# A longer hand-fixed order of VectorE and ScalarE through two products, spatial turns ahead of the first logits, and one addition ordered behind a norm

## The chip, the cores and the metric

The kernel runs on one core of a Trainium2 chip. The metric is the device time of one execution in microseconds, as the median of several runs. TensorE (PE) multiplies matrices and transposes tiles into PSUM, VectorE (DVE), ScalarE (ACT) and GpSimd (POOL) do elementwise work, and SyncE (SP) issues most DMAs; ScalarE issues a few. Every engine works through its own queue in order and waits for others by semaphores.

## What is computed

A decoder block on a sequence of 1024 tokens of width 1024, in float32: a norm, one projection, two groups of heads beside each other (attention with a forget gate, and a causal spatial gating), an output projection, and a gated MLP of width 2816 with a short causal convolution.

```
xn = rmsnorm(h);  proj = xn @ w_in            # q, k, v, u, vg, forget gate
att = forgetting_attention(q, k, v, log_f)    # 8 heads of 64, causal
sg  = u * (tril(w_s) @ rmsnorm(vg) + b_s)     # in chunks of 128 tokens; u, vg = gelu(proj)
h = h + concat(att, sg) @ w_out
h = h + conv_ffn(rmsnorm(h))                  # (silu(g) * a) @ w_down behind a causal conv of width 3
out = rmsnorm(h)
```

## The kernel before

**Numbers.** TensorE multiplies fp32r values here. To hold float32 accuracy each operand is split into a high part (a cast, on ScalarE) and a low part (the value less the cast, on VectorE), and a product is three matmuls: high by high, high by low, low by high. Thus every operand costs ScalarE a cast and VectorE a subtraction before TensorE can start on it. `tsplit` (line 242) splits a weight tile into one of six buffers that are used in a ring (`RTAG`, line 196); `own` (207) splits an x tile and scales it by the norm's gain; `hl_of` (213) splits two x tiles at once; `tmul` (249) does the 12 matmuls of one 128-row step k of a product, and `tprod` (258) does four of these steps, each with its split.

**Products.** The large products are done in Strassen's manner in Winograd's form: 2x2 blocks, seven products instead of eight, with sums of blocks on either side. The x blocks and their sums are named B11, B21, B22 and T1 to T4; the weight sums S1 to S4. The first stage (lines 219 to 408) is the projection to u and vg. Its product results go to two sets of four PSUM banks, `B` and `S`, which are exchanged after T2. From there the order of TensorE is T3 (banks S), T1 (banks B, 48 matmuls), T4 (added into S), B22 (added into B), and then the value products of the second token half (`values_high`, line 472), the queries and keys (`qk_step`, 588).

- `ut[1]` is bank B (of T2) less `vgt[0]`, and has to be read before T1 overwrites B. `vgt[1]` is `ut[1] + S`, less B after T1.
- `gb[k]` holds two weight blocks; T1 takes their sum, T4 the second one alone.
- `tmp[j]` holds x differences. `tmp[j][0]` is the source of T1, `tmp[j][1]` that of T4 (after one more operation with x21, the `t2` lines), `tmp[j][2]` that of B22. `tmp[1][1]` and `tmp[1][2]` lie in the buffer that `vgt[1]` takes later.
- `squares(tt)` (line 317) loads a token tile from `xtok` on SyncE and has ScalarE add up its squares; two load buffers are used in turn. From the eight sums, `rstd1` (a square root on ScalarE, a reciprocal on VectorE) is made; it is needed by the gelus, and as `rb`, stored by ScalarE's DMA to `rbd` and loaded back as a row by SyncE, for the queries and keys.

**The order.** The program's instructions are placed in each engine's queue by a scheduler with its own cost model. The class `Line` (line 28) wraps ScalarE, VectorE and GpSimd: while `on` is true, every instruction of that engine is tied behind the one before it, so the engine keeps the written order; once it is off, later instructions are only tied behind the last of the fixed ones. In the kernel before, the order of ScalarE and VectorE is fixed from the start to B22's splits (line 365) and is free from there, so T1 and T4 with their splits are placed by the scheduler. A trace shows instructions of a fixed order at L51 and those after it at L44, whatever line called them.

**The spatial turns.** After attention's inputs are ready, the spatial gating (`spatial`, 722) leaves its output in `ut[0]` and `ut[1]`; the latter is multiplied by GpSimd (L752). `turn_sg(hf, c, ps)` (761) transposes four blocks of it on TensorE into one bank, and `sg_hi` and `sg_lo` split the result into `sgT` (tag G). Then a new PSUM pool has two buffers "L" of two banks each for logits: `logits_mm(h, j, ps)` (898, matmuls L907 and L908) computes query block j of a head, `logits_min` (912) reads it on VectorE and sets the buffer free, and `logits_exp` runs on ScalarE. `firsts` holds the buffers of blocks 7 and 6; block 5 takes that of block 7. `seq` fixes the order of TensorE here, and the fixed order of ScalarE and VectorE holds too.

**The second norm.** After attention, `wmm` (1174) does the output projection of one token tile, `hadd` (1186) adds the half result to the rest of the residual stream, which `hload` has loaded, `norm2` (1190) norms the tile, and `flip` (1207) transposes it (L1214) for the next product. The tiles come in the order 0, 4, 1, 5, 2, 3, 6, 7, and a tile is flipped after the next one's norm is written. The order of VectorE is free here.

## Time and profile before

| | us |
|---|---|
| median of 3 runs | 1063.64 |
| lowest and highest run | 1061.78, 1063.86 |
| profiled execution | 1064.82 |
| its span, first to last instruction | 1063.1 |
| TensorE busy | 1048.1 (99%) |
| VectorE busy | 886.9 (83%) |
| ScalarE busy | 571.2 (54%) |
| GpSimd busy | 234.5 (22%) |

A row of a list of instructions reads: start, busy time, engine, line, operation, tile written <- tiles read, shape, count, and in brackets the engine's idle time just before with what ended it. Rows of one kind in a row are merged, so the time of a row with x4 is that of four. Tile names are without their numbers: "wy" and "whl" are the ring of weight splits, "H", "V", "x" and "t" hold x operands, "pb" and "ps" are PSUM banks, "pl" the logits' buffers. A row of the waits names who waited, for whom, then the total, the times and the longest. A row of the stretches gives start:end, length, the busy time and instructions of PE, PE's weight loads, DVE, ACT and POOL, then PEclk, the TensorE clock granted (1.00 is full), the DMA share and GB/s.

### The profile page before, as it was taken

The page shows a single profiled execution, that of the slowest core. Times are in us where ns is not written, and L with a number is a line of the kernel's source. Part 1 is how long each engine was busy: PE and PEld are TensorE (multiplying, and loading weights), DVE is VectorE, ACT ScalarE, POOL GpSimd, SP SyncE. Part 2 cuts the span into 40 slices and gives each one's busy share as a digit, 9 for nine tenths or more (in the row PEclk, how much of TensorE's full clock was granted, in tenths as well). Part 3 has the DMA queues.
Part 4 walks back from the last instruction along what each step waited for, and adds up shares of the span by engine and source line. Part 5 has one row for each costly group of instructions (what it writes and reads, how often), then busy time and mean ns, then how long its engine had stood idle before and what let it go on. Part 6 is the DMA issues. An engine that isn't in the chain of part 4 may idle for free.

```text
span 1063.1 us, 14614 instructions
## 1 busy us (share of the span) xinstructions
PE 1048.1 (99%) x5156; PEld 881.9 (83%) x5156; DVE 886.9 (83%) x1297; ACT 571.2 (54%) x1013; POOL 234.5 (22%) x177
## 2 busy tenths in 40 slices
PE   9989999999999999999999999999999999999997
PEld 7978888988889887878888888888888888888885
DVE  6899697877877869998999989989898866997774
ACT  6667534465866846754434444444444544554653
POOL 0003141330420740153333433323321000000000
PEclk9999999999999999999999999999999999999999
DMA  9613365857565444223245323332322899333432
GB/s 338 201 28 113 104 172 155 228 156 193 152 180 159 139 158 169 75 84 108 90 149 176 132 100 100 109 108 80 129 100 77 291 331 304 115 100 99 142 119 96
DMA packets 67184, 155.78 MB, mean 147 GB/s; under 512 B 9028, under 2 KB 9748, under 8 KB 67112
## 3 DMA queue, kind: packets, MB, share of 16 engines
q1 hardware_dynamic: 65800, 154.82, 45.6%
q8 instruction: 40, 0.66, 0.3%
q14 instruction: 32, 0.26, 0.1%
q10 hardware_dynamic: 1312, 0.04, 0.1%
HBM read 111.96 MB, written 42.87 MB: 146 GB/s over the span
## 4 chain that ended last, share of the span: by engine, by line
PE 87%; DVE 7%; DMA 3%; ACT 2%; issue 1%; SPq 0%; DVEq 0%; ACTq 0%
PE k L1527 20%; PE qa L1269 11%; PE qc L1269 11%; PE qd L1269 10%; PE qb L1269 5%; PE ps L259 4%; PE pb L966 3%; PE pb L947 3%; PE pb L259 2%; PE qa L418 2%; PE qc L418 2%; PE qd L418 2%; PE pl L907 2%; PE pl L908 2%; PE pf L991 1%; PE pf L993 1%
## 5 line engine op out<-in xcount | busy, mean ns | idle before, releaser
L1527 PE MATMUL k<-whb,wha 128*128 128x512 f32 x924 | 209.8, 389 | 0.0
L1527 PEld LDWEIGHTS k<-whb,wha 128*128 128x128 f32 x924 | 173.4, 188 | 36.2 <-DVE wha L161 0.2
L1269 PE MATMUL qc<-xT,whb 128*128 128x512 f32 x540 | 129.9, 390 | 0.5 <-DVE u L1380 0.5
L1269 PE MATMUL qa<-xB,wha 128*128 128x512 f32 x528 | 127.2, 390 | 0.0
L1269 PEld LDWEIGHTS qc<-xT,whb 128*128 128x128 f32 x540 | 101.3, 188 | 22.0 <-DVE u L1380 0.9
L1269 PEld LDWEIGHTS qa<-xB,wha 128*128 128x128 f32 x528 | 98.8, 188 | 20.8 <-DVE wha L161 0.4
L155 ACT CAST wha<-sg 128x512 fp32r<-128x512 f32 x77 | 47.8, 622 | 97.0 <-PE k L1527 86.4
L155 ACT CAST whb<-sg 128x512 fp32r<-128x512 f32 x82 | 50.5, 617 | 87.1 <-PE qc L1269 68.7
L161 DVE TENSOR_TENSOR wha<-sg,wha 128x512 fp32r<-128x512 f32 x77 | 52.8, 688 | 40.0 <-ACT wha L155 39.9
L948 ACT CAST pt<-pb 128x512 fp32r<-128x512 f32 (+1 forms) x80 | 42.2, 544 | 43.1 <-PE pb L947 34.2
L1269 PE MATMUL qd<-xB,whb 128*128 128x512 f32 x264 | 63.9, 390 | 0.1
L1269 PE MATMUL qd<-xT,whb 128*128 128x512 f32 x264 | 63.6, 389 | 0.0
L161 DVE TENSOR_TENSOR whb<-sg,whb 128x512 fp32r<-128x512 f32 x82 | 57.7, 705 | 4.4 <-ACT whb L155 4.3
L1269 PE MATMUL qb<-xT,whb 128*128 128x512 f32 x252 | 60.8, 389 | 0.0
L1156 POOL TENSOR_TENSOR sg<-raw 128x512 f32<-128x512 f32 x20 | 30.2, 1512 | 136.7 <-DVE whb L161 75.7
L949 DVE TENSOR_TENSOR pt<-pb,pt 128x512 fp32r<-128x512 f32 (+1 forms) x80 | 48.8, 635 | 12.3 <-ACT pt L948 11.0
L1269 PEld LDWEIGHTS qd<-xB,whb 128*128 128x128 f32 x264 | 49.5, 188 | 10.8 <-DVE h L1388 0.5
L1269 PEld LDWEIGHTS qd<-xT,whb 128*128 128x128 f32 x264 | 49.6, 188 | 10.3
L1269 PEld LDWEIGHTS qb<-xT,whb 128*128 128x128 f32 x252 | 47.3, 188 | 9.8
L966 PE MATMUL pb<-pt,V 128*128 128x256 f32 x320 | 52.1, 288 | 0.3 <-DVE pt L949 0.2
L1159 POOL TENSOR_TENSOR sg<-sg,raw 128x512 f32<-128x512 f32 x20 | 33.3, 1664 | 64.4 <-DVE whb L161 64.4
L1157 POOL TENSOR_TENSOR sg<-sg,raw 128x512 f32<-128x512 f32 x20 | 34.8, 1742 | 50.7 <-issue 48.8
(404 smaller groups left out, 2287.0 us busy)
## 6 DMA issues: line engine op xcount, KB each, us to landing
raw<-wup SPq DMA_DIRECT2D x44, 512.0 KB
sg<-hx SPq DMA_DIRECT2D x77, 256.0 KB
hx<-hs SPq DMA_DIRECT2D x44, 256.0 KB
hx<-ca SPq DMA_DIRECT2D x35, 256.0 KB
xT<-wdn SPq DMA_DIRECT2D x28, 256.0 KB
x<-kd SPq DMA_DIRECT2D x24, 256.0 KB
A<-xtok SPq DMA_DIRECT2D x8, 512.0 KB
raw<-wqk SPq DMA_DIRECT2D x8, 512.0 KB
```

The source lines that it names most:

```text
L155: act.copy(h, src)
L161: return eng.tensor_tensor(out=l, in0=src, in1=f32(h), op=ALU.subtract)
L259: pe.matmul(banks[m], xs(n, xi, k)[:, ms], w[:, wi, :], start=(first and k == 0 and c == 0 and (own or m % 2 == 0)), stop=(k == 3 and c == ...
L418: pe.matmul(ps, w[:, wi, ks], xs(n, xi, k), start=(first and c == 0), stop=(c == 11), skip_group_check=True)
L947: seq(pe.transpose(ptr[:, c:c + P], tj[jj][:, k * P:(k + 1) * P], ident))
L948: casts.append(act.copy(pt[:, 0, 0:w], ptr[:, 0:w]))
L949: los.append(dve.tensor_tensor(out=pt[:, 1, 0:w], in0=ptr[:, 0:w], in1=f32(pt[:, 0, 0:w]), op=ALU.subtract))
L966: seq(pe.matmul(po[0][:, oo:oo + n], lhs, pt[:, s, o:o + n], start=(k == 0 and s == 0), stop=(s == 1 and half)))
L1157: pool.tensor_tensor(out=s[1], in0=s[0], in1=a11, op=ALU.add)
L1159: pool.tensor_tensor(out=s[3], in0=s[1], in1=a12, op=ALU.add)
L1269: pe.matmul(ps, w[:, wi, ks], xb[:, xi, k, :], start=(first and n == 0), stop=(n == 11), skip_group_check=True)
L1527: pe.matmul(banks[bk + m], xh[:, xi, ms], wh[:, wi, :], start=(first and p_ == 0 and n == 0), stop=(p_ == NP - 1 and n == 2), skip_group_c ...
```

## The change

The diff has four parts.

1. The fixed order of ScalarE and VectorE goes on through T1 to the splits of T4. In it the weight sums of `gb` come right after T3's splits, then T1's own splits, with squares(6) and squares(7) between them and the `ut[1]` subtractions ahead of the last of them, then the weight splits for T1, and with them the root for `rstd1`. The gelus of `ut[0]`, the `t2` operations and T4's splits follow, still fixed. The store to `rbd` and the load of `rb` come after the fixed order.
2. `ut[1] + S` is written to a new tile `mid` in the buffer of tag t3 instead of `vgt[1]`, ahead of T4's splits. B22's first half uses that same single buffer, so its split comes after `mid` has been read; B22's second half is split after the fixed order. The two `sum4` come there too.
3. All four turns of the second half of the spatial output come ahead of the logits of blocks 7 and 6, instead of two turns, block 7, two turns, block 6.
4. VectorE's `hadd` of tile 5 is tied behind the last operation of the norm of tile 1.

```diff
             tmul(S, tsplit(ua[k][:, 0, :]), "T3", k, True)
-        squares(5 + j)
-    squares(7)
-    XS["B22"] = xset(("t3", "t2"))
-    for j in range(2):
-        hl_of("B22", j, tmp[j][2])
-    act.on = dve.on = False
-    for m in range(4):
-        dve.tensor_tensor(out=ut[1][:, m, :], in0=B[m], in1=vgt[0][:, m, :], op=ALU.subtract)
+        if j == 0:
+            squares(5)
     for w in gb:
         dve.tensor_tensor(out=w[:, 0, :], in0=w[:, 0, :], in1=w[:, 1, :], op=ALU.add)
-    XS["T1"] = xset(("H", "H"))
+    XS["T1"], mid = xset(("H", "H")), sb("t3", [P, 4, 512])
+    for k in range(4):
+        if k == 3:
+            for m in range(4):
+                dve.tensor_tensor(out=ut[1][:, m, :], in0=B[m], in1=vgt[0][:, m, :], op=ALU.subtract)
+        own("T1", tmp[k // 2][0][:, k % 2], k, k)
+        if k in (1, 2):
+            squares(5 + k)
+    for k in range(4):
+        tmul(B, tsplit(gb[k][:, 0, :]), "T1", k, True)
+        if k == 1:
+            act.activation(rstd1, ss1, AF.Sqrt, bias=eps[:, 0:1], scale=1.0 / 1024)
+            dve.reciprocal(rstd1, rstd1)
+    for m in range(4):
+        gelu(ut[0][:, m, :], m)
+    for k in range(4):
+        t2 = tmp[k // 2][1][:, k % 2]
+        dve.scalar_tensor_tensor(out=t2, in0=xr("x21", k), scalar=gk(4 + k), in1=t2, op0=ALU.mult, op1=ALU.subtract)
+    for m in range(4):
+        dve.tensor_tensor(out=mid[:, m, :], in0=ut[1][:, m, :], in1=S[m], op=ALU.add)
+    XS["T4"] = xset(("V", "V"))
     for j in range(2):
-        for c in range(2):
-            own("T1", tmp[j][0][:, c], 2 * j + c, 2 * j + c)
-
-
-    act.activation(rstd1, ss1, AF.Sqrt, bias=eps[:, 0:1], scale=1.0 / 1024)
-    dve.reciprocal(rstd1, rstd1)
+        hl_of("T4", j, tmp[j][1])
+        for k in (2 * j, 2 * j + 1):
+            tmul(S, tsplit(gb[k][:, 1, :]), "T4", k, False)
+    act.on = dve.on = False
     rb = sb("t01", [P, 1024])
     act.dma_start(out=rbd.rearrange("a p -> p a"), in_=rstd1)
     sp.dma_start(out=rb, in_=rbd.rearrange("a b -> (a b)").unsqueeze(0).to_broadcast((P, 1024)))
-
-    tprod(B, lambda k: gb[k][:, 0, :], "T1", True)
-    for m in range(4):
-        gelu(ut[0][:, m, :], m)
+    XS["B22"] = xset(("t3", "t2"))
+    hl_of("B22", 1, tmp[1][2])
     sum4(2)
     sum4(3)
-    for m in range(4):
-        dve.tensor_tensor(out=vgt[1][:, m, :], in0=ut[1][:, m, :], in1=S[m], op=ALU.add)
...
     for m in range(4):
-        dve.tensor_tensor(out=vgt[1][:, m, :], in0=vgt[1][:, m, :], in1=B[m], op=ALU.subtract)
+        dve.tensor_tensor(out=vgt[1][:, m, :], in0=mid[:, m, :], in1=B[m], op=ALU.subtract)
+    hl_of("B22", 0, tmp[0][2])
     tprod(B, lambda k: ua[k][:, 1, :], "B22", False)
...
     for c in range(4):
         pts.append(turn_sg(1, c, bank()))
-        if c % 2:
-            logits_mm(0, 7 - c // 2, firsts[7 - c // 2])
+    for j in (7, 6):
+        logits_mm(0, j, firsts[j])
...
     def hadd(tt, hf, ps):
         o = slice(hf * 512, hf * 512 + 512)
-        dve.tensor_tensor(out=h2[tt][:, o], in0=ps, in1=h2[tt][:, o], op=ALU.add)
+        x = dve.tensor_tensor(out=h2[tt][:, o], in0=ps, in1=h2[tt][:, o], op=ALU.add)
+        if tt == 5:
+            after(tc, x, normed[1])
```

The first `...` leaves out the removed lines with the `t2` operations, T4's splits and T4's product in their old place; `normed[tt]` holds the last VectorE operation of `norm2(tt)`.

More of the change, by code (lines that the diff above doesn't have):

```diff
@@ L380, in block_kernel @@
     sp.dma_start(out=rb, in_=rbd.rearrange("a b -> (a b)").unsqueeze(0).to_broadcast((P, 1024)))
-    tprod(B, lambda k: gb[k][:, 0, :], "T1", True)
-    for m in range(4):
-        gelu(ut[0][:, m, :], m)
+    XS["B22"] = xset(("t3", "t2"))
+    hl_of("B22", 1, tmp[1][2])
     sum4(2)
     sum4(3)
-    for m in range(4):
-        dve.tensor_tensor(out=vgt[1][:, m, :], in0=ut[1][:, m, :], in1=S[m], op=ALU.add)
-    for j in range(2):
-        t2 = tmp[j][1]
-        for c in range(2):
-            k = 2 * j + c
-            dve.scalar_tensor_tensor(out=t2[:, c], in0=xr("x21", k), scalar=gk(4 + k), in1=t2[:, c],
-                                     op0=ALU.mult, op1=ALU.subtract)
-    XS["T4"] = xset(("V", "V"))
-    for j in range(2):
-        hl_of("T4", j, tmp[j][1])
-    tprod(S, lambda k: gb[k][:, 1, :], "T4", False)
     wh = []
@@ L1172, in block_kernel @@
     xn = [None] * 8
+    normed = {}
     def wmm(tt, hf, ps, ks_):
@@ L1195, in norm2 @@
         dve.reciprocal(r, r)
-        dve.scalar_tensor_tensor(out=xn[tt], in0=h2[tt], scalar=r, in1=g2b, op0=ALU.mult, op1=ALU.mult)
+        normed[tt] = dve.scalar_tensor_tensor(out=xn[tt], in0=h2[tt], scalar=r, in1=g2b, op0=ALU.mult, op1=ALU.mult)
         sp.dma_start(out=h2d[tt], in_=h2[tt])
```

## The prediction, made before the result was known

> **What bounds the kernel now.** I read the head of the page first, then TensorE's waits, then the stretch around the longest of them.

> ```profile
> span 1063.1 us, 14614 instructions
> ...
> PE 1048.1 (99%) x5156; PEld 881.9 (83%) x5156; DVE 886.9 (83%) x1297; ACT 571.2 (54%) x1013; POOL 234.5 (22%) x177
> ```

> TensorE is busy for 1048.1 of 1063.1 us. The change removes no matmul, so it can save only TensorE's idle time (15.0 us in all, most of it at the two ends) and what slow clock follows from it. The list of who made TensorE wait shows which of that is within reach (total us, times, longest):

> ```profile
> PE ps L259 <- DVE wy L44: 3.1, 1, 3.1
> PE ps L122 <- DVE pad L133: 1.3, 1, 1.3
> PE ps L1214 <- DVE xn L1196: 0.9, 1, 0.9
> PE pb L947 <- DVE pt L949: 0.8, 2, 0.5
> PE pl L907 <- DVE G L51: 0.7, 1, 0.7
> ```

> Rows one, three and five are the three places that the diff touches: the start of product T1, the flip of token tile 1 after the second norm, and the first logits after the spatial turns. The stretches around the first one (start:end, length, busy times, then PEclk, the granted clock):

> ```profile
> 50.21:61.09 10.88, 10.88 (x50) 9.01 (x49) 7.78 (x12) 9.05 (x14) 0.00 (x0) 1.00 0.06 25
> 62.16:65.26 3.10, 0.00 (x0) 0.00 (x0) 3.10 (x7) 1.64 (x4) 0.00 (x0) 1.00 0.00 0
> 65.26:67.92 2.66, 2.66 (x8) 2.10 (x9) 2.66 (x5) 2.65 (x4) 0.00 (x0) 0.71 0.18 2
> 67.92:76.99 9.07, 9.07 (x37) 7.42 (x36) 8.26 (x13) 4.79 (x7) 0.00 (x0) 0.90 0.11 7
> 76.99:87.87 10.88, 10.88 (x49) 9.01 (x48) 10.88 (x15) 6.98 (x11) 3.97 (x4) 1.00 0.80 255
> ```

> T3 (48 matmuls) takes 10.88 us, T4 too. T1, between them, has the same 48 matmuls and takes 76.99 - 61.09 = 15.90. So the wait costs 15.90 - 10.88 = **5.02 us**, not 3.10: after it TensorE has a granted clock of 0.71 for 2.66 us and of 0.90 for 9.07 us, which is 0.29 x 2.66 + 0.10 x 9.07 = 1.68 us lost; the last 0.24 is the restart.

> Why T1 waits is read on VectorE, which is busy through the whole wait:

> ```profile
> 54.73 1.23 DVE L51 TENSOR_TENSOR t<-pt,t 128x1024 fp32r<-128x1024 f32 x1 [3.10 <-ACT t L51]
> 55.87 1.22 DVE L51 TENSOR_TENSOR t<-G,t 128x1024 fp32r<-128x1024 f32 x1
> 57.01 2.48 DVE L44 TENSOR_TENSOR A<-ps,G 128x512 f32<-128x512 f32 x4
> 59.40 2.49 DVE L44 TENSOR_TENSOR G<-G 128x512 f32<-128x512 f32 x4
> 61.81 1.41 DVE L44 SCALAR_TENSOR_TENSOR H<-pt,g,H 128x512 fp32r<-128x512 f32 x2
> 63.13 1.41 DVE L44 SCALAR_TENSOR_TENSOR H<-t,g,H 128x512 fp32r<-128x512 f32 x2
> 64.46 0.19 DVE L44 RECIPROCAL rstd<-rstd 128x8 f32<-128x8 f32 x1
> 64.57 0.64 DVE L44 TENSOR_TENSOR wy<-G,wy 128x512 fp32r<-128x512 f32 x1
> ```

> It sat idle from 51.63 to 54.73, then did B22's two splits (not needed before 87.87), the four ut[1] subtractions, the four weight sums, T1's four own splits, the reciprocal, and only then the weight split T1 waits for. ScalarE caused the idle time, in the fixed order, with the load for squares(7):

> ```profile
> 49.59 0.62 ACT L51 CAST wy<-raw 128x512 fp32r<-128x512 f32 x1
> 50.11 1.06 ACT L51 ACTIVATE A<-A 128x1024 f32<-128x1024 f32 x1
> 51.07 0.19 ACT L51 ACTIVATION_READ_ACCUMULATOR A<-A 128x1 f32 x1
> 52.61 1.06 ACT L51 ACTIVATE A<-A 128x1024 f32<-128x1024 f32 x1 [1.35 <-DMA A<-xtok]
> ```

> **The change, part by part.** *T1.* I put the new fixed order on the old clock. From the starts above, one of a row costs VectorE 0.60 us (four sums or subtractions in 2.39, or a split), 0.66 (an own split) and 1.14 (a 1024-wide split). T3's last split ends at 51.63 in both kernels. Then: sums of gb to 54.0; own splits 0 to 2 to 56.0; ut[1] subtractions to 58.4; own split 3 to 59.1; weight split of gb[0] to **59.7**. T3 ends at 61.09, so T1 finds everything ready with 1.4 us to spare; gb[1] follows at 60.3 and is needed at 61.09 + 2.72 = 63.8. ScalarE has to be ahead. Its last T3 cast ends at 50.1; own casts 0 and 1 (0.62 each) to 51.35, squares(6) to 52.4, own cast 2 to 53.0, squares(7) (load there at 52.6, issued as before, since squares(5) stays where it was) to 54.1, own cast 3 and the first two gb casts to 56.0. Each is before VectorE's use. So both the 3.10 us and the slow clock go: **-5.02**.

> What is late next? T4, which now begins at 71.97. VectorE from 59.7: three gb splits and the reciprocal to 61.6, four t2 operations to 64.3, four additions into mid to 66.7 (T3 is done by 61.5), T4's first 1024-wide split to 67.8, its first weight split to 68.4: 3.5 us early. On ScalarE these wait for the gelus, and those for the reciprocal:

> ```profile
> 65.10 1.28 ACT L44 ACT_TABLE_LOAD   x1 [1.46 <-DVE rstd L44]
> 66.39 2.56 ACT L44 ACTIVATE A<-A,rstd 128x512 f32<-128x512 f32 x4
> ```

> With the reciprocal at about 60.5, load and gelus end at 64.3, T4's first cast (two of 0.62 at most) at 65.5, before VectorE's 66.7. Then B22 at 82.85. Its first half must now wait until mid, which holds the one t3 buffer, has been read: T1's end at 72.2, four subtractions 2.4, a cast of up to 1.24, a split of 1.14, so 77.0 at the earliest; 5.9 us to spare. The buffers of the splits are a ring of six filled in the same order as before, so no split waits for another matmul.

> Queues: the rbd store moves behind the fixed order on ScalarE, and the load of rb on SyncE waits for it, with the wv loads behind:

> ```profile
> 64.68 0.39 ACTq L44 DMA_DIRECT2D rbd<-rstd  x1
> ```
> ```profile
> 74.03 0.33 SPq L380 DMA_DIRECT2D t<-rbd  x1
> 75.30 3.92 SPq L403 DMA_DIRECT2D G<-wv  x4
> ```

> 9.35 us lie from the store to the load of rb. With the store at about 68.5 the wv loads go out at about 78 to 82, some 3 us later than now, for values that TensorE takes up behind B22, now at 87.87 + 10.88 = 98.75, then at 93.7: hidden, and it would cost only the part of a delay beyond some 7 us. Bounds for the T1 part: a gain of 5.02 at most, and nothing if T4 or B22 takes the wait over.

> *Turns.* Transposes (L767), the first logits (block 7, 219.53) and the third (block 5, 222.26), with the pieces beside them on GpSimd and VectorE:

> ```profile
> 217.78 1.06 PE L767 MATMUL pb<-ident,A 128*128 128x128 f32 x8
> 219.53 0.50 PE L907 MATMUL pl<-x 128*128 128x512 f32 x1 [0.69 <-DVE G L51]
> ...
> 222.26 0.40 PE L907 MATMUL pl<-x 128*128 128x512 f32 x1
> ```
> ```profile
> 213.52 5.58 POOL L752 TENSOR_TENSOR A<-pt,A 128x256 f32<-128x256 f32 x8
> ```
> ```profile
> 220.76 1.28 DVE L51 CUSTOM_DVE_ANT_0 t<-pl,t,lim 128x1024 f32<-128x1024 f32 x1 [0.69 <-PE pl L908]
> ```

> The eight transposes that now stand between blocks 7 and 6 take up to 1.06 us and go into the gap of 0.69 ahead of block 7, so TensorE is through block 6 by about 0.8 us earlier. But block 5 takes the buffer of block 7, which is free only when VectorE's 1.28 us operation on block 7 is through, at 222.04, and that operation starts behind block 7, which hardly moves. Block 5 starts at 222.26 now, so the wait goes from the first block of L907 to the third. The turns of c = 3 also need GpSimd's eighth product, which ends at 219.10; TensorE gets there twelve transposes behind 217.78, at about 219.0 to 219.4, and that can push block 7 by 0.1 to 0.3 us. I take **0.0**, from -0.2 (222.26 becomes 222.1) to +0.3, nearest to what the buffer allows.

> *Addition.* At the second norm, TensorE then VectorE:

> ```profile
> 403.80 1.06 PE L1214 MATMUL ps<-ident,xn 128*128 128x128 f32 x8 [0.92 <-DVE xn L1196]
> ```
> ```profile
> 400.59 0.16 DVE L1195 RECIPROCAL ss<-ss 128x1 f32<-128x1 f32 x1
> 401.77 0.69 DVE L1188 TENSOR_TENSOR pt<-pb,pt 128x512 f32<-128x512 f32 x1 [1.02 <-DMA pt<-hpd]
> 402.38 1.27 DVE L1196 SCALAR_TENSOR_TENSOR xn<-pt,ss,g2b 128x1024 f32<-128x1024 f32 x1
> ```

> VectorE holds for hadd(5), which waits 1.02 us for its load, with the norm of tile 1 ready behind it. With the norm first it runs at 400.75 to 402.0, ahead of TensorE, which is free at 403.80 - 0.92 = 402.88; hadd(5) starts at 401.95, its load having landed, 0.18 later than now, while all that stands behind the pair starts about 1.0 us earlier. The gain on TensorE is 0.92 and up to 0.2 of restart, and no more than the 1.0 that VectorE gains, since flips and norms alternate from here to the next product: **-1.0** (bounds 0 and -1.1).

> Sum: -5.0 + 0.0 - 1.0 = -6.0. The profiled execution took 1064.82 us (its span 1063.1 and 1.7 around it), so 1058.8; the median of the runs, 1063.64, is 1.2 lower, which gives **1057.6 us**.

> **Rivals.** *The clock dips without the wait.* No other wait of this trace is above 1.3 us and none but this one has a clock under 1.00 behind it within the stages read, which speaks for the wait as the cause; but there is only this one case. If the dip stays, T1 gains only about 3.1 + 0.2 and the time is 1057.6 + 1.7 = 1059.3.
> [...]

> *VectorE in the fixed order is later than worked out* by 2 us or more (a semaphore's delay at each of some 25 steps). T1 has 1.4 us to spare, so a wait of about 1 us stays, or T4 gets it: half of the T1 part, 1060.1.

> *B22's first half is late (slower).* Behind the fixed order the program places VectorE's work freely, and VectorE was busy 10.88 of 10.88 us in T4's stretch. If over 5.9 us of other work (weight splits, square sums, the gate's reductions) stands ahead of mid's subtractions and B22's split, TensorE waits at 82.85, and a wait costs 5.02 / 3.10 = 1.6 per us with the clock. It eats the whole gain at 3.7 us of wait; from 5.1 us on the kernel is slower by over 0.2%: about 1066. Against it: mid's subtractions come ahead of the other work in the program, and what is left for that stretch is worth about 8 us.

> *Nothing changes:* T1's wait only moves to T4, 1063.

> **How the numbers follow.** Forecast 0.64 (its own range 1056.3 to 1058.9: the bounds of turns and addition, and the 1 us that the three runs lie from their middle); the clock 0.12 (1059.3); VectorE late 0.08 (1060.1); nothing 0.06 (1063); slower 0.10 (1066). A measurement of this kernel can tell about 0.2% (2.1 us) from no change. Faster: 0.64 + 0.12 + 0.08 = 0.84; same 0.06; slower 0.10. The range reaches over the first three cases: 1056.3 to 1061.0.

> **What would show it.** TensorE's 3.1 us wait at L259 for the wy split gone, T1 in about 10.9 us, granted clock 1.00 from 50 to 75 us, and every later stage 5.0 us earlier. At the turns, a wait of about 0.7 us at L907 for VectorE's minimum in place of the one for G. No wait of L1214 for xn at tile 1, and 1.0 us more between spatial turns and first up-projection. I am wrong if a product from T1 to B22 waits for VectorE, if the clock dips anyway, or if VectorE's free order after the fixed one lets a later product wait.

## The result, and the profile after

| | before | after |
|---|---|---|
| median of 6 runs each | 1062.71 us | 1058.90 us |
| lowest to highest | 1061.48 to 1064.18 | 1058.51 to 1059.72 |
| profiled execution, its span | 1064.82, 1063.1 | 1059.72, 1058.0 |

The ratio is 0.9965, with a 95% interval of 0.9952 to 0.9977: 3.7 us faster (2.4 to 5.1). The forecast was 1057.6 within 1056.3 to 1061.0, so the time lies in the range, 1.3 us above the forecast, and the gain is 3.7 us where 6.0 were worked out. Two things have to be explained: which parts brought it, and where the other 2.3 us are.

TensorE's waits in the changed kernel, in the form who waited, for whom, total us, times, longest:

```profile
PE ps L122 <- DVE pad L133: 1.3, 1, 1.3
PE pb L259 <- ACT wy L51: 1.0, 1, 1.0
PE pb L946 <- DVE pt L948: 0.8, 2, 0.5
PE pl L906 <- DVE mn L51: 0.6, 1, 0.6
PE pb L259 <- DVE wy L51: 0.3, 1, 0.3
PE pb L965 <- DVE pt L948: 0.2, 1, 0.2
PE qc L1271 <- ACT whb L155: 0.2, 1, 0.2
```

The 3.1 us for the wy split at T1 and the 0.9 us for xn at tile 1 are gone. The row of the logits now names the minimum (mn) in place of the split G. The two L259 rows are at the very first products (6.2 and 9.8 us after the start), where nothing was changed: in this one execution ScalarE waits 1.1 us for the first wuv load, for which it has no wait in the profile of before, and T3 begins at 51.24 us, 1.03 us later than in the profile of before. T3, T1 and T4 in the changed kernel, as stretches:

```profile
51.24:62.12 10.88, 10.88 (x49) 9.01 (x48) 10.88 (x20) 10.13 (x17) 0.00 (x0) 1.00 0.07 26
62.12:73.00 10.88, 10.88 (x49) 9.01 (x48) 10.88 (x16) 7.59 (x12) 0.00 (x0) 1.00 0.30 3
73.00:83.88 10.88, 10.88 (x49) 9.01 (x48) 10.53 (x15) 7.37 (x11) 1.50 (x2) 1.00 0.68 131
```

T1 now takes 10.88 us like its neighbours, at a granted clock of 1.00. VectorE in its fixed order, from T3's last split to T1's splits:

```profile
51.98 0.68 DVE L51 TENSOR_TENSOR wy<-raw,wy 128x512 fp32r<-128x512 f32 x1
52.58 2.49 DVE L51 TENSOR_TENSOR G<-G 128x512 f32<-128x512 f32 x4
54.99 1.41 DVE L51 SCALAR_TENSOR_TENSOR H<-pt,g,H 128x512 fp32r<-128x512 f32 x2
56.31 0.74 DVE L51 SCALAR_TENSOR_TENSOR H<-t,g,H 128x512 fp32r<-128x512 f32 x1
56.98 2.47 DVE L51 TENSOR_TENSOR A<-ps,G 128x512 f32<-128x512 f32 x4
59.37 0.74 DVE L51 SCALAR_TENSOR_TENSOR H<-t,g,H 128x512 fp32r<-128x512 f32 x1
60.03 0.68 DVE L51 TENSOR_TENSOR wy<-G,wy 128x512 fp32r<-128x512 f32 x1
```

There is no idle time in it, and T1's weight split ends at about 60.7, 1.4 us ahead of T1, the spare time that the prediction gave. (Other executions have more or less, as the section on the length of a wait shows.) The turns, TensorE first:

```profile
213.92 2.22 PE L766 MATMUL pb<-ident,A 128*128 128x128 f32 x16
215.89 0.48 PE L906 MATMUL pl<-x 128*128 128x512 f32 x1
...
218.46 0.50 PE L906 MATMUL pl<-x 128*128 128x512 f32 x1 [0.55 <-DVE mn L51]
```

All sixteen transposes come first and block 7 starts without a wait, but block 5 then waits 0.55 us. From the start of the first turns to block 5 it was 222.26 - 216.03 = 6.23 us before and is 218.46 - 212.17 = 6.29 now. The second norm, VectorE and then TensorE:

```profile
396.80 0.16 DVE L1197 RECIPROCAL ss<-ss 128x1 f32<-128x1 f32 x1
396.99 1.28 DVE L1198 SCALAR_TENSOR_TENSOR xn<-pt,ss,g2b 128x1024 f32<-128x1024 f32 x1
398.20 0.68 DVE L1229 TENSOR_TENSOR t<-xtB,ps 128x512 f32<-128x512 f32 x1
398.79 0.68 DVE L1230 TENSOR_TENSOR t<-xtB,xtB 128x512 f32<-128x512 f32 x1
399.40 0.68 DVE L1188 TENSOR_TENSOR pt<-pb,pt 128x512 f32<-128x512 f32 x1
```
```profile
398.43 1.07 PE L1216 MATMUL ps<-ident,xn 128*128 128x128 f32 x8
```

The norm comes right behind its reciprocal, the flip follows without a wait, and hadd(5) comes two operations later still.

Where the difference of the two profiled spans, -5.1 us, comes from, by the starts of the same products on TensorE: +1.03 from the first loads, -5.02 at T1, +0.13 up to the spatial turns, +0.06 at the turns, -0.8 from flips and norms to the first up-projections (436.91 to 432.33, where flip 0 had gone from 396.64 to 392.85), +0.7 in the second step of the up-projection and -1.2 in its third, where before a product waited 0.5 us for VectorE and restarted. The last two belong to the tie of hadd(5): all nine profiles of kernels with the tie have them, and none of the five without it. The first loads apart, the difference is -6.1 us, next to the -6.0 of the sum. So the sum was about right for the one execution that it was made from, though partly by luck, since the last two were not in it and nearly make up for a smaller gain at the flips. The kernel's other runs are not all like that one.

### The profile page after: what moved, and what is told of

Its sections match the earlier page's. It is cut to its first block, busy times and chain, and to the rows that moved or that the text cites. A ratio compares the mean times of both kernels' runs of the same rounds, so it can differ in the third digit from the quotient of the medians.

```text
span 1058.0 us, 14612 instructions
## 1 busy us (share of the span) xinstructions
PE 1046.3 (99%) x5156; PEld 880.3 (83%) x5156; DVE 884.0 (84%) x1297; ACT 571.1 (54%) x1013; POOL 235.8 (22%) x177
## 4 chain that ended last, share of the span: by engine, by line
PE 94%; DVE 2%; DMA 1%; ACT 1%; POOL 1%; issue 0%; SPq 0%; POOLq 0%; ACTq 0%; DVEq 0%
PE k L1529 20%; PE qc L1271 11%; PE qa L1271 11%; PE qd L1271 11%; PE ps L259 5%; PE qb L1271 5%; PE pb L259 5%; PE pb L965 3%; PE pb L946 3%; PE qa L417 2%; PE qc L417 2%; PE qd L417 2%; PE pl L906 2%; PE pl L907 2%; PE pf L990 1%; PE pf L992 1%
## 5 line engine op out<-in xcount | busy, mean ns | idle before, releaser
L947 ACT CAST pt<-pb 128x512 fp32r<-128x512 f32 (+1 forms) x80 | 42.2, 544 | 43.1 <-PE pb L946 34.2
L1158 POOL TENSOR_TENSOR sg<-sg,raw 128x512 f32<-128x512 f32 x20 | 33.0, 1650 | 63.8 <-DVE whb L161 63.8
L965 PEld LDWEIGHTS pb<-pt,V 128*128 128x128 f32 x320 | 43.8, 190 | 2.6 <-DVE pt L948 0.4
```

The source lines that it names most:

```text
L947: casts.append(act.copy(pt[:, 0, 0:w], ptr[:, 0:w]))
L965: seq(pe.matmul(po[0][:, oo:oo + n], lhs, pt[:, s, o:o + n], start=(k == 0 and s == 0), stop=(s == 1 and half)))
L1158: pool.tensor_tensor(out=s[3], in0=s[1], in1=a12, op=ALU.add)
```

## The experiments

Each kernel is timed beside the kernel before. One us is 0.094% of the time.

### One part at a time, and the kernel before itself

```diff
e1_before: no change
e2_order:  parts 1 and 2 of the change (fixed order, mid); turns and hadd as before
e3_turns:  before with
-        if c % 2:
-            logits_mm(0, 7 - c // 2, firsts[7 - c // 2])
+    for j in (7, 6):
+        logits_mm(0, j, firsts[j])
e4_hadd:   before with
+        if tt == 5:
+            after(tc, x, normed[1])
```

> The kernel before, unchanged. Theory A (the clock dip after T1's wait does not come in every execution): its times fall into two groups some 1.7 to 2.2 us apart, about 1061.6 and 1063.9, the lower group with the higher mean granted clock. Rival B (the dip always follows the wait; the two groups come from the first loads): the clock is the same in both groups, and a profile shows 0.7 and 0.9 behind T1's wait whatever its time.

> The long fixed order with mid alone; turns and hadd as in the kernel before. Theory (as predicted): T1 in 10.9 us without a wait and without a dip, 3.1 to 5.0 us faster than the kernel before depending on whether that one dips; the median about 4 us lower. Rival: the order alone gains less than 3 us, and the rest of the change's gain is that of turns and hadd.

> The four turns ahead of the logits alone. Theory: no difference (0.0, from -0.2 to +0.3 us): the 0.7 us wait of TensorE at the first logits becomes a wait of 0.5 to 0.7 us for VectorE's minimum at the third. Rival: the wait goes, 0.7 to 0.9 us faster.

> The tie of hadd(5) behind the norm of tile 1 alone. Theory: the flip of tile 1 comes without its 0.9 us wait, 0.8 to 1.0 us by the first up-projection; what the free order of the later splits makes of it is worth as much again in either direction, so -2 to 0 us at the end. Rival: the scheduler's new order gives it all back, 0.0.

| kernel | median us | ratio, 95% interval | TensorE's wait at T1 in its profile |
|---|---|---|---|
| e1_before | 1063.18 | 1.0001, 0.9991 to 1.0011 | 2.6 |
| e2_order | 1060.07 | 0.9969, 0.9958 to 0.9980 | none |
| e3_turns | 1063.24 | 1.0000, 0.9990 to 1.0009 | 1.6 |
| e4_hadd | 1062.56 | 0.9989, 0.9980 to 0.9998 | 2.1 |

The order brings 3.3 us (2.1 to 4.5), less than the 4 that I expected, the norm 1.2 (0.2 to 2.1), the turns nothing (-1.0 to 1.1). The three add up to 4.5 us, the whole change brought 3.7; the difference is within the intervals. e3's row of the waits shows the exchange that was expected:

```profile
PE pl L907 <- DVE mn L51: 0.6, 1, 0.6
```

The kernel before was executed 31 times beside these four. Sorted by time, 15 executions lie at 1061.43 to 1062.38 us with a mean granted clock of 0.998 or 0.999, then there is a gap, and 16 lie at 1063.49 to 1065.82 with 0.995 to 0.997. The medians of the two groups are 1062.07 and 1063.98, 1.9 us apart; the dip behind T1's wait had been worked out as 1.68. That is theory A of the first expectation. The gap is less clear elsewhere: e1_before itself has runs at 1062.96 and 1063.40. Over all four rounds of experiments, 40 of 81 executions of the kernel before have a clock of 0.998 or more and take 1061.04 to 1063.29 us, and 41 have 0.997 or less and take 1063.31 to 1065.82; their medians, 1062.05 and 1063.99, are again 1.9 us apart. The profile of e1_before caught an execution at 1062.47 us with a clock of 0.998. Its T1, as the first four matmuls with the wait, the next eight, and the other 36:

```profile
61.44:65.11 3.67, 1.07 (x5) 0.56 (x4) 3.67 (x8) 2.21 (x5) 0.00 (x0) 1.00 0.00 0
65.11:67.06 1.95, 1.95 (x9) 1.61 (x10) 1.95 (x4) 1.94 (x3) 0.00 (x0) 1.00 0.24 2
67.06:75.22 8.16, 8.16 (x38) 6.76 (x37) 8.16 (x12) 5.41 (x8) 0.00 (x0) 1.00 0.00 0
```

The same instructions, a wait of 2.6 us, and a clock of 1.00 behind it; T1 takes 13.78 us here, not 15.90. Nor is the wait the same each time. Four profiles with the old order give, in us:

| | squares(7) starts on ScalarE | behind T3's start | T1 goes on | behind squares(7) | T1's wait |
|---|---|---|---|---|---|
| before | 52.61 | 2.40 | 65.26 | 12.65 | 3.1 |
| e1_before | 52.45 | 1.89 | 65.11 | 12.66 | 2.6 |
| e4_hadd | 51.53 | 1.43 | 64.19 | 12.66 | 2.1 |
| e3_turns | 51.24 | 0.87 | 63.91 | 12.67 | 1.6 |

In all four T1 goes on 12.65 to 12.67 us behind squares(7), so its wait grows with the lateness of squares(7) against T3 (the wait is 0.7 us longer in each). That operation waits for its load in all four profiles, but ScalarE's idle time for it does not tell the lateness: it is 1.35 us in the first profile and 0.43 to 0.46 in the other three, whose waits still differ by 1.0 us. The load goes out when squares(5) has freed its buffer (in before at 48.25 us, where squares(5) with its sum is through at 48.23), and squares(5) itself starts 2.75 to 3.73 us ahead of T3; from the issue of the load to squares(7) it is 4.3 us in the first profile and 3.4 in the others. The profile that the prediction was made from has both the longest wait of the four and, alone among them, the dip.

### How long a wait is, and what the clock makes of it

VectorE gets n more subtractions of 0.60 us, repeats of the four that are there, ahead of T1's last own split in the changed kernel:

```diff
             for m in range(4):
                 dve.tensor_tensor(out=ut[1][:, m, :], in0=B[m], in1=vgt[0][:, m, :], op=ALU.subtract)
+            for m in range(n):
+                dve.tensor_tensor(out=ut[1][:, m % 4, :], in0=B[m % 4], in1=vgt[0][:, m % 4, :], op=ALU.subtract)
```

> The changed kernel with two of the four ut[1] subtractions done twice on VectorE ahead of T1's last own split (2 x 0.60 = 1.2 us later; same values). Theory: inside the 1.5 us that VectorE has to spare ahead of T1, so no wait at T1 and the time of the changed kernel, 1058.9. Rival (VectorE has nothing to spare): 1.2 us slower.

> Five such subtractions more (3.0 us): T1 waits 3.0 - 1.5 = 1.5 us. Theory (a short wait does not lower the clock): +1.5 us, about 1060.4, one group of times, granted clock 1.00 behind the wait. Rival (any wait here costs 1.6 us per us): +2.4, about 1061.3.

> Eight (4.8 us): T1 waits 3.3 us, as in the first profile of the kernel before. [...]

> Twelve (7.2 us): T1 waits 5.7 us. Theory: the dip in every execution, 5.7 + 1.7 to 3.4: 1066.3 to 1068.0. Rival (no dip from a wait): 1064.6.

| n | T1 in the profile, over 10.88 | median us | ratio, 95% interval | executions at a clock of 0.997 or less |
|---|---|---|---|---|
| 2 | +0.4 | 1058.89 | 0.9964, 0.9951 to 0.9978 | 0 of 4 |
| 5 | +0.7 | 1059.60 | 0.9969, 0.9958 to 0.9980 | 0 of 7 |
| 8 | +2.2 | 1061.37 | 0.9989, 0.9981 to 0.9998 | 3 of 11 |
| 12 | +7.1 | 1066.49 | 1.0032, 1.0020 to 1.0045 | 5 of 5 |

My numbers for the waits of d5 and d8 were too high, d2 loses 0.4 us where none was expected, and most executions of d8 were expected to have the dip, where 3 of 11 have it. The spare time, expected as 1.5 us, is not one number: VectorE is earlier or later against T3 from one execution to the next. T1's weight split ends 1.4 us ahead of T3's end in the first profile of the changed kernel and 2.8 us ahead in the second (a1_after). With the spare time of each profiled execution (in us; what the split would have had without the added work) the four come out:

| n | added | spare without it | split late by | matmuls of T1 ahead of the split | left to wait | T1 over 10.88 |
|---|---|---|---|---|---|---|
| 2 | 1.2 | 0.7 | 0.5 | 1 (0.2 us) | 0.2 | 0.4 |
| 5 | 3.0 | 1.8 | 1.2 | 3 (0.7) | 0.5 | 0.7 |
| 8 | 4.8 | 1.8 | 3.0 | 4 (0.9) | 2.0 | 2.2 |
| 12 | 7.2 | 1.4 | 5.8 | 4 (0.9) | 4.9 | 7.1 |

The matmuls ahead of the split need only the high parts; how many there are differs from kernel to kernel. In d8 and d12 the added subtractions also hold these four back, because they read the banks B that T1 overwrites: the four start 0.6 us apart, like the subtractions. So TensorE's delay there is not one wait. In d8 the longest idle time is 0.76 us, in d12 2.72.

In d12, 2.2 us are left over, and the clock accounts for them. When it falls can be read from the granted clock that the traces of these runs record. From its first rise to its fall at the program's end it has only the values 1.00 and 0.50 in all 14 profiles, and the times between its changes are whole multiples of 3.41 us: 3.41 and 6.83 at 0.50, and 58.03 (17 times), 61.44 (18), 989.87 (290), 1047.89 (307) and 1051.31 (308) at 1.00. In before, for one, it rises at 4.95 us, falls at 66.39, rises at 69.80 and falls at 1059.67; in the changed kernel it rises at 4.17 and falls at 1055.47. So all its changes in these profiles lie at the ends of steps of 3.41 us counted from the first rise, and that comes 4.2 to 7.3 us after the start, at another place in each execution. The steps around the fall in before and d12, the step with the most idle time that has no fall behind it, in e1_before, and the step with the least that has one, at the very end of e2_order:

```profile
62.98:66.39 3.41, 1.13 (x5) 0.94 (x6) 3.41 (x8) 1.94 (x3) 0.00 (x0) 1.00 0.14 1
66.39:69.80 3.41, 3.41 (x10) 2.65 (x9) 3.41 (x7) 3.29 (x6) 0.00 (x0) 0.50 0.00 0
```
```profile
61.60:65.02 3.42, 0.68 (x2) 0.19 (x1) 3.42 (x7) 0.00 (x0) 0.00 (x0) 1.00 0.00 0
65.02:71.84 6.82, 6.34 (x13) 4.37 (x14) 6.82 (x12) 3.66 (x6) 0.00 (x0) 0.50 0.00 0
```
```profile
63.28:66.69 3.41, 1.58 (x7) 1.32 (x8) 3.41 (x7) 1.94 (x3) 0.00 (x0) 1.00 0.14 1
```
```profile
1050.09:1053.50 3.41, 1.39 (x7) 0.81 (x5) 2.85 (x8) 2.54 (x7) 0.00 (x0) 1.00 0.40 163
```

TensorE was idle for 2.28 us of the step before the fall in before and for 2.74 in d12. At the end of the program, the last step ahead of the fall has 2.02 us in e2_order and 2.62 or more in the other 13 profiles (all of its 3.41 in before and in the changed kernel). No step with 1.83 us or less, the one of e1_before among them, has a fall behind it. One step at half the clock costs 3.41 / 2 = 1.7 us, the 1.68 of the prediction. In d12 it stayed at 0.50 for two steps, of which the part behind 67.49, when T1 runs without a wait again, costs 0.50 x (71.84 - 67.49) = 2.2 us; before that the four matmuls are held back by the subtractions anyway.

My reading is that a fall depends on how much of a wait falls into one step, and not on the length of the wait alone: e1_before's wait of 2.6 us was divided by the end of a step at 63.28, into 0.77 and 1.83. In these profiles the most idle time in a step without a fall behind it is 1.83 us, and the least with one 2.02. That the wait of 2.6 us would have had the dip with the steps placed otherwise would follow from the reading but is not shown, since no two profiles have the same wait and a different clock. Over many executions, the order of before has the dip in about half of them (16 of the 31), d8 in 3 of 11, d12 in all 5, d5 in none of 7.

### Is it the load, or the order?

```diff
-    squares(7)
     XS["B22"] = xset(("t3", "t2"))
     for j in range(2):
         hl_of("B22", j, tmp[j][2])
+    squares(7)
     act.on = dve.on = False
```

This moves one operation of ScalarE and leaves the rest of the kernel before as it is (e5_sq7); e6_short adds the tie of hadd(5).

> The kernel before with squares(7) moved behind B22's two splits, still in the fixed order; nothing else. Theory (T1's start hangs on the load for squares(7): in four profiles of the old order it comes 12.66 us after squares(7) starts): VectorE's 2.2 to 3.1 us of idle time ahead of B22's splits goes, T1 waits for 0.3 us or less and the clock never dips; 2 to 4 us faster than the kernel before, about 1060.1, like the long fixed order alone. Rival (the order of VectorE's work is the bound, not the load): T1 still waits over 1 us, under 1 us gained.

> The same with hadd(5) tied behind the norm of tile 1. Theory: the two gains add, 1.2 us faster than squares(7) alone: 1058.9, the time of the changed kernel. Rival: the long order gains more than the wait alone, and this one stays 1 us behind the changed kernel.

> The changed kernel again, beside these two: 1058.9 by the theory, all runs in one group with a mean granted clock of 0.998 or more.

e5_sq7 took 1061.21 us (ratio 0.9984, 0.9976 to 0.9993), e6_short 1060.27 (0.9975, 0.9965 to 0.9984), the changed kernel 1058.92 beside them (0.9964, 0.9951 to 0.9976). VectorE at B22's split in e5_sq7, and TensorE's waits at L259:

```profile
52.19 1.22 DVE L51 TENSOR_TENSOR t<-pt,t 128x1024 fp32r<-128x1024 f32 x1 [0.60 <-ACT t L51]
```
```profile
PE ps L259 <- DVE wy L44: 1.0, 1, 1.0
...
PE pb L259 <- DVE whl L44: 0.3, 1, 0.3
```

VectorE's idle time shrinks from 3.10 to 0.60 us, no execution of the 11 (or of e6's 9) has a clock under 0.998, and 1.7 us (0.7 to 2.6) of the order's 3.3 are gained: the place of squares(7) is about half of the story. The move takes two things from ahead of B22's split, the wait for the load and the 1.05 us that squares(7) itself takes on ScalarE; how much of the gain is due to each was not tried. And T1 still waits for 1.0 us (0.3 in e6's profile), because B22's two splits, which nobody needs yet, and T1's weight split keep their places; and a later value product waits 0.3 us for its split. My theory gave a wait of 0.3 us or less and 1060.1 for e5_sq7, and 1058.9 for e6_short, and fell there. The long order is worth another 1.35 us (1060.27 less 1058.92), as the rival of e6_short said. Counted by the starts on TensorE from T3 on, e6_short is 0.6 us behind the changed kernel at the end of T1, and the later wait with its restart adds 0.5.

### A version without the wait at block 5

```diff
+    dve.on = False
+    fill((-1, 5))
+    dve.on = True
     logits(0, 5)
+    after(tc, added[0], dve.last)
     sg_lo(1, 3, pts[3])
     act.on = dve.on = False
     act.last = dve.last = None
-    fill((-1, 5))
```

(`added` holds the additions of `sg_out`.)

> The changed kernel with the first 12 matmuls of the spatial output projection (L990 to L992, 2.8 us) put ahead of the logits of block 5 instead of behind them, and their addition on VectorE tied behind block 5's minimum. Theory (block 5 waits for its buffer, which block 7's minimum sets free): TensorE's wait of 0.55 us for VectorE's minimum goes, and the stretch from the spatial turns to the first value product is 0.5 us shorter at most; 1058.4, not to be told from 1058.9 by the time alone. Rival (VectorE's chain of minima and splits is the bound of this stretch): the wait comes back at the logits of block 3, nothing gained.

It took 1059.99 us (0.9971, 0.9959 to 0.9982). By the medians that is 1.1 us slower than the changed kernel, by the ratios 0.7, with intervals that overlap; but all its 7 executions (1059.78 to 1060.36) lie above all 12 of the changed kernel (1058.51 to 1059.72). TensorE:

```profile
PE pf L992 <- DVE G L51: 1.2, 1, 1.2
...
PE pl L906 <- DVE mn L51: 0.5, 1, 0.5
```

The 12 matmuls wait for VectorE's split into the tiles G, and later a block of logits waits for a minimum again (at 222.73 us, block 3). The rival was right: VectorE's chain of minima and splits is what this stretch hangs on, and the two waits together (1.2 and 0.5 us) cost more than the one (0.6 in the changed kernel). From the first turns to the first transposes for a value product (L946) it is 18.4 us here and 17.3 in the changed kernel. No version was found that beats the changed kernel.

## Why the prediction was right, and what was off

- *T1's wait goes, with its clock:* right, step by step. VectorE's order, the 1.4 us to spare at T1's start and the stretch of 10.88 us came as worked out. **Off was the size of this term.** 5.02 us is true of the profiled execution; over many it is 3.3 (e2_order), because the wait is 1.6 to 3.1 us in four profiles, set by how late squares(7) is against T3, and the dip comes in about half of the executions. The error lay in taking one profiled execution as the typical one and then only moving its sum by 1.2 us onto the median. The three runs shown already lay at 1061.78, 1063.64 and 1063.86: one of the lower group and two of the upper.
- *T4 and B22 take nothing over:* right. T4 follows T1 without a gap and all waits of the early products but those of the first loads are gone. The rival of a late B22 did not occur, nor that of VectorE being late; the spare time of 1.4 us was again that of one execution, and the other profiles of the changed order without added work have 1.8 (f1_fill), 2.0 (e2_order) and 2.8 (a1_after).
- *The rival on the clock:* in the form "the dip stays without the wait" it is refuted, since no execution of the changed kernel, e2_order, e5_sq7, e6_short, f1_fill, d2 or d5, whose profiles have a wait of 1.0 us or less at T1, shows a clock under 0.998. The reverse happened, the wait without the dip: it is 2.6 us in e1_before's profile at a clock of 1.00, and 40 of 81 executions of the kernel before have a clock of 0.998 or more. The rival's 1059.3 is nearer to the 1058.9 than the forecast is, by luck as far as its own mechanism goes. The spread of the three runs would have justified more than the 0.12 that it had.
- *The turns:* right, with the mechanism: ratio 1.0000 (e3_turns), the wait moved from block 7 to block 5.
- *The addition:* right in size by the time, 1.2 us (0.2 to 2.1) against 1.0. In the trace, 0.8 of it is there by the first up-projections. The rest, +0.7 and -1.2, comes in the up-projection with every kernel that has the tie, and the prediction had not counted it; that it is the scheduler's new placing of free instructions is argued, not shown.
- *Queues:* the later store to rbd and load of rb delayed no product, as costed: the load went out at 78.0 us, and TensorE has no wait between 80 and 200 us.
- *The range:* the forecast's own upper end, 1058.9, leaves out the case that the addition brings nothing; with it, its terms give 1059.9. The time of 1058.90 lies just at this end; the range to 1061.0 was wider because it was drawn over two rivals, neither of which came true as it was written.

What stays open: why the load for squares(7) took 0.9 us longer in one profile, and why ScalarE and VectorE stand earlier or later against T3 from one execution to the next, was not tried; nor was the load of squares(7) changed without moving its 1.05 us on ScalarE.

## What to carry to other kernels

Before the price of a wait is taken from one profile, look at the spread of the runs: if they fall into groups, the profile shows one of them, and the mean granted clock tells which (here 0.998 or more in the one group, 0.997 or less in the other). A wait of TensorE can hang on a load through a chain of other engines, and has to be traced back along it; here moving one operation with its load gave about half of the gain of the order (1.7 of 3.3 us), and the order of the engine behind it the rest. Moving the transposes into the gap ahead of block 7 gained nothing here (ratio 1.0000, e3_turns), because block 5 then waited 0.6 us for its buffer, which VectorE's minimum sets free.
